# Up projections with both parts of x as one moving operand, and tiles placed at round addresses

## The chip, the cores and the metric

The kernel runs on one core of one Trainium2 chip. The metric is the device time of one execution in microseconds, the lower the better. A core has TensorE (PE in the profile; its weight loads are listed apart as PEld), VectorE (DVE), ScalarE (ACT), GpSimd (POOL) and SyncE (SP), which here only issues transfers. Each engine works through its own queue in order and waits on semaphores for the others.

## The reference: what is computed

Two layers of an encoder over 256 positions with 1024 channels, all in float32. Each layer has a token-mixing part (one input projection, a Hyena long convolution, a gated linear attention, a pooling mixer, three gated branch projections, one output projection, each with RMS norms around it) and a channel-mixing part. The change is in the channel-mixing part:

```python
h = _rms_norm(x, norm_ffn_pre[i])
a, b = _split(h @ ffn_w_up[i], (D_FF, D_FF))          # D_FF = 2816
a = _dwconv3_centred(a, ffn_conv_w[i], ffn_conv_b[i])  # three taps along the positions
y = (jax.nn.gelu(a, approximate=False) * b) @ ffn_w_down[i]
x = x + _rms_norm(y, norm_ffn_post[i])
```

## The kernel before

**Two parts of every number.** To keep float32 accuracy with TensorE's faster float32r format, each operand is cut into a high part (rounded to float32r) and a low part (what is left). A product then takes three matmuls: high by high, high by low, low by high (`mm3`, line 128).

**Weights.** All weight matrices are cut into 71 chunks a layer, each 128 partitions by 2048 numbers, 1 MB (line 31). SyncE loads them in the order of use into three raw buffers (`dma_next`, line 183). Each half of a chunk is split: ScalarE copies the high part into a slot (`split_upper`, line 205), VectorE subtracts it from the raw data to make the low part (`split_lower`, line 222); when both halves are done the raw buffer takes the next load. `filler` (line 246) splits ahead of use, as far as `ahead["chunks"]` and the free slots allow.

**Slots.** SBUF for passing data is a set of 37 big slots of 4096 bytes a partition (`b` in the profile) and 9 small ones of 2048 (`s`), PSUM is 8 banks (`p`); `Slots` (line 59) hands out the slot that has been free for the longest. The transposed and normalised activations, x, live in four big slots: two with the high and two with the low part, each for four blocks of 128 channels by 256 positions (`xt_alloc`, line 549). They are held while a layer's projections read them; `xt` is for token mixing, `xt2` for channel mixing, `xt3` for the next layer.

**The order of the work.** `unit` (line 320) emits the matmuls of one step, then the steps that empty the banks of the unit before it (`pending`), then lets the side work go on (`tick`) and splits weights ahead (`filler`). `cost` says how much side work a unit makes room for: 2.6 stands for one step. Side work beside the up projections of layer 0 is the Hyena filter of layer 1 (`filt`, line 467). A planner that simulates the engines puts the emitted instructions into each engine's order; in some windows the written order is kept (`open_window`, line 135).

**Up projections.** Line 1180 runs over 11 pairs in `UP_ORDER`; a pair is 256 channels of the gate path `a` and 256 of `b`. The `a` chunk goes through `two_ftiles` (line 576): two tiles of 128 output channels, one after the other in the two halves of one PSUM bank, each with 8 steps of the contraction and three matmuls in a step, weights stationary (128x128) and x moving (256 positions). Then `a_post` reads PSUM three times for each tile (`conv3`: one ScalarE step, two VectorE steps) and applies the GELU. For pairs 4 to 10 the `b` chunk goes the same way and `b_post` multiplies and splits. For pairs 0 to 3 the `b` channels come from four chunks computed just before the loop with x stationary, and are only transposed (line 1204). So each layer has 11 + 7 = 18 chunks through `two_ftiles` here; token mixing uses `two_ftiles` for other chunks, which the change leaves as they are. The down projection (line 1225) follows, with 512 moving columns of weights.

Of the kernel before, what the change touches and what calls it, by code (L numbers as in the profile page):

```python
# [12 lines left out]
F32 = mybir.dt.float32  # L13
# [70 lines left out]
@with_exitstack  # L84
def trunk(ctx: ExitStack, tc: tile.TileContext, a: dict, out: bass.AP):
    nc = tc.nc
    cpool = ctx.enter_context(tc.tile_pool(name="cst", bufs=1))
    wpool = ctx.enter_context(tc.tile_pool(name="wts", bufs=3))
    spool = ctx.enter_context(tc.tile_pool(name="slt", bufs=1))
    ppool = ctx.enter_context(tc.tile_pool(name="psm", bufs=1, space=bass.MemoryType.PSUM))  # L90
    big = Slots(spool, "b", 37, 4096)
    sml = Slots(spool, "s", 9, 2048)
    psm = Slots(ppool, "p", 8, 2048)

# [10 lines left out]
    def act(o, i, func=AF.Copy, **kw):  # L105
        ins = nc.scalar.activation(o, i, func, **kw)  # L106
        if func in TABLED:
            tc.stamp_issue_order_token(ins.ins, TOKEN)
# [10 lines left out]
    def mm(o, w, x, start, stop):  # L119
        ins = nc.tensor.matmul(o, w, x, start=start, stop=stop).ins  # L120
        if not isinstance(ins, tuple):
            newest["pe"] = ins
# [127 lines left out]
    def weights(n, at, width):  # L250

        half, at = divmod(at, 1024)
        return wh[n][half][:, at:at + width], wl[n][half][:, at:at + width]
# [39 lines left out]
    def start(gen, lift=0):  # L293
        s = Side(gen, lift)
        sides.append(s)
        return s

    def tick():
        for s in list(sides):
            s.step()  # L300
            if s.done:
                sides.remove(s)
# [244 lines left out]
    handles = {}  # L547

    def xt_alloc():
        return ([big.get([P, 4, L], F32R) for _ in range(2)], [big.get([P, 4, L], F32R) for _ in range(2)])  # L550

    def chunk_x_stationary(n, xt, t, o, half, first=None, lows_late=False):

# [14 lines left out]
            mm(o, x[:, k, s], l if m == 1 else h, half == 0 and (k, m) == todo[0], half == 1 and (k, m) == todo[-1])  # L568

    def ftile(n, xt, f, o, width=256, kn=8):  # L570
        xth, xtl = xt
        for k in range(kn):
            h, l = weights(n, k * width + f * P, P)
            mm3(o, h, l, xth[k // 4][:, k % 4, :], xtl[k // 4][:, k % 4, :], k == 0, k == kn - 1)

    def two_ftiles(n, xt, post):
        ps = psm.get([P, 2, L])
        unit([n], lambda: ftile(n, xt, 0, ps[:, 0, :]))

        def fin():  # L580
            post(ps)
            psm.put(ps)

        unit([n], lambda: ftile(n, xt, 1, ps[:, 1, :]), fin, free=n)
# [6 lines left out]
    def layer(i, xt, chains):  # L591
# [4 lines left out]
        def take():  # L596
            n = nxt()
            cur["c"] += 1
            return n
# [466 lines left out]
        def branch(b, ready):  # L1066
            for half in range(2):
                gate = room([P, 2, 512])
                if b == 0:
                    merged.append(gate)  # L1070
                n0, n1 = take(), take()
                for t in range(2):
                    ps = psm.get([P, 512])

                    def post(ps=ps, t=t, gate=gate):
                        act(gate[:, t, :], ps[:], AF.Sigmoid)
                        psm.put(ps)
                    for j, nj in enumerate((n0, n1)):
                        unit([nj, n1 if t else n0], lambda: chunk_x_stationary(nj, xt, t, ps[:], j),
                             post if j else None, free=nj if t else None)  # L1080
                ys = ready()
                n = take()
                if b == 2 and half == 1:
                    flush()
                    big.put(*xt[0], *xt[1])
                if b == 2:
                    mhl[half] = big.get([P, 4, L], F32R), big.get([P, 4, L], F32R)
                for t in range(2):
                    ps = psm.get([P, 512])

                    def post(ps=ps, gate=gate, half=half, t=t):
                        g, m = gate[:, t, :], merged[half][:, t, :]
                        tt(g, g, ps[:], ALU.mult)
                        psm.put(ps)
                        if b > 0:
                            tt(m, m, g, ALU.add)
                            if t == 1:
                                big.put(gate)
                        if b == 2:
                            later.append(lambda: merge_up(half, t))  # L1100

                    def pe(ps=ps, t=t):
                        s = slice(t * P, (t + 1) * P)
                        for k in range(4):
                            h, l = weights(n, k * 512, 512)
                            mm(ps[:], ys[0][:, k, s], h, k == 0, False)
                            mm(ps[:], ys[0][:, k, s], l, False, False)
                            mm(ps[:], ys[1][:, k, s], h, False, k == 3)
                    unit([n], pe, post, free=n if t else None)
# [29 lines left out]
        for t in range(2):  # L1139
            banks = [psm.get([P, 512]) for _ in range(2)]  # L1140
            ready = [False, False]
            ch2.append(start(post_norm(t, banks, g_post_t, g_pre2, *xt2, ready), LIFT))
            for c in range(4):
                def fin(ready=ready, c=c):
                    ready[c // 2] = True
                unit(ns[:c + 1] if t == 0 else ns[c:],
                     lambda: chunk_x_stationary(ns[c], mx, t, banks[c // 2][:], c % 2),
                     fin if c % 2 else None, free=ns[c] if t else None)
                if t == 0 and c == 2:
                    open_window()  # L1150
# [29 lines left out]
        for pair in UP_ORDER:  # L1180
            if pair // 2 not in ys_h:
                ys_h[pair // 2] = big.get([P, 4, L], F32R)
                ys_l[pair // 2] = big.get([P, 4, L], F32R)
            ga = sml.get([P, 2, L])

            def a_post(ps, pair=pair, ga=ga):
                for j in range(2):
                    conv3(ga[:, j, :], ps[:, j, :], i, V_FFC + 4 * (pair * 2 + j))
                act(ga[:], ga[:], AF.Gelu)

            def b_post(ps, pair=pair, ga=ga):
                tt(ga[:], ga[:], ps[:], ALU.mult)
                s = slice((pair % 2) * 2, (pair % 2) * 2 + 2)
                split(ys_h[pair // 2][:, s, :], ys_l[pair // 2][:, s, :], ga[:])
                sml.put(ga)
            two_ftiles(take(), xt2, a_post)
            if pair >= NB:
                two_ftiles(take(), xt2, b_post)
            else:
                ps = psm.get([P, 2, L])  # L1200
                for j in range(2):
                    f = (pair * 2 + j) * P
                    for t in range(2):
                        nc.tensor.transpose(ps[:, j, t * P:(t + 1) * P], bt[t][:, f:f + P], ident[:])  # L1204
                flush()

                def fin(ps=ps, b_post=b_post, pair=pair):
                    b_post(ps)
                    psm.put(ps)
                    if pair == NB - 1:  # L1210
                        big.put(*bt)
                pending.append(fin)
# [32 lines left out]
        for at, (t, c) in enumerate(seq):  # L1245
            if not done_first and c == 1:
                done_first = True
                flush()
                big.put(*xt2[0], *xt2[1])
                xt3 = xt_alloc() if not last else (None, None)  # L1250

            def fin(t=t):
                ch3.append(start(post_norm(t, banks[t], g_post2, None if last else g_cur["pre"], *xt3), LIFT))
            oldest = min(cc for _, cc in seq[at:])
            if t == 0 and c == 7 and not last:
                open_window()
            unit([ns[c], ns[oldest]], lambda: down(t, c), fin if c == 10 else None, free=ns[c] if t else None)
            if t == 1 and (c % 2 or c == 10):
                big.put(ys_h[c // 2], ys_l[c // 2])
        if last:  # L1260
            ready = [False, False]
            ch3.append(start(post_norm(1, banks[1], g_post2, None, *xt3, ready)))
            tail = [(half, c) for half in range(2) for c in range(11 - LEAD, 11)]
            for half, c in tail:
                def fin(half=half):
                    ready[half] = True
                unit([ns[c]], lambda: down(1, c, (half,)), fin if c == 10 else None, cost=1.3)
# [240 lines left out]
```

## Time and profile before

| | |
|---|---|
| time, median of 3 runs | 884.92 us (884.22 to 886.0) |
| the profiled execution | 884.6 us, its span 882.8 us |
| mean granted TensorE clock | 0.996 of full |
| matmuls, weight loads | 5381, 5381 |
| busy: TensorE, VectorE, ScalarE, GpSimd | 872.6, 636.0, 512.4, 37.4 us |
| read from HBM | 161.54 MB, 184 GB/s over the span |

A line of the profile names the engine, the line of the kernel (often that of a helper: L120 is every matmul, L106 every ScalarE step, L111 every VectorE step on two tensors, L114 every VectorE step with a scalar and two tensors, L374 and L1204 are transposes), the tiles written and read, the shapes, and how often it occurs. "Idle before" is the time in which the engine stood still ahead of these instructions, with what ended it. In tables by stretches each engine's busy time stands with the number of its instructions in brackets.

### The profile page before, as it was taken

How to read it: one execution, taken by the hardware profiler on the slowest of the kernel's cores; microseconds unless marked ns; L12 is line 12 of the kernel's file. 1: busy time of each engine (PE TensorE's matmuls, PEld its weight loads, DVE VectorE, ACT ScalarE, POOL GpSimd, SP SyncE). 2: the span in 40 equal slices, each digit the busy share in tenths (PEclk: the TensorE clock that was granted, in tenths of full speed). 3: DMA queues.
4: the chain of work that ended last, by engine and by line, in shares of the span. 5: the costliest groups of instructions: out<-in, count | busy, mean ns of one | idle time of the engine just before them, and what ended most of it. 6: DMA issues, size and time to landing. Idle time of an engine off the chain costs nothing.

```text
span 882.8 us, 13499 instructions
## 1 busy us (share of the span) xinstructions
PE 872.6 (99%) x5381; PEld 783.1 (89%) x5381; DVE 636.0 (72%) x925; ACT 512.4 (58%) x809; POOL 37.4 (4%) x86
## 2 busy tenths in 40 slices
PE   9999999999999999999999999999999999999997
PEld 7899987888888999998889999888888899999885
DVE  7899988766586798665288989876755967776612
ACT  7779666555365776554268865864543665555501
POOL 3000100000010000000010000000000000000000
PEclk9999999999999999999999999999999999999999
DMA  9854535746546446466349453465752674445501
GB/s 319 336 192 170 168 105 190 241 144 238 191 163 244 143 136 246 149 222 226 120 136 338 175 160 131 153 198 177 279 184 81 236 284 143 166 173 199 204 1 48
DMA packets 48431, 163.46 MB, mean 185 GB/s; under 512 B 3442, under 2 KB 29189, under 8 KB 33520
## 3 DMA queue, kind: packets, MB, share of 16 engines
q1 hardware_dynamic: 44352, 151.69, 49.2%
q0 software_dynamic: 4000, 10.90, 3.9%
q8 instruction: 42, 0.69, 0.3%
q14 instruction: 21, 0.17, 0.1%
q10 hardware_dynamic: 16, 0.00, 0.0%
HBM read 161.54 MB, written 1.05 MB: 184 GB/s over the span
## 4 chain that ended last, share of the span: by engine, by line
PE 96%; DVE 2%; DMA 1%; ACT 0%; issue 0%; SPq 0%; DVEq 0%; POOLq 0%; POOL 0%; ACTq 0%
PE p L120 94%; DVE b L111 1%; DMA raw<-in_wts 1%; PE p L374 1%; PE p L1059 0%; PE p L1204 0%; DMA x<-in_x 0%; ACT b L106 0%; PE p L775 0%; PE p L876 0%; PE p L1021 0%; DVE b L114 0%; DVE b L1281 0%; DVE s L111 0%; PE p L1294 0%
## 5 line engine op out<-in xcount | busy, mean ns | idle before, releaser
L120 PE MATMUL p<-b,b 128*128 128x256 f32 (+2 forms) x5022 | 842.1, 328 | 2.6 <-DVE b L111 1.9
L120 PEld LDWEIGHTS p<-b,b 128*128 128x128 f32 x5022 | 740.9, 190 | 85.6 <-DVE b L111 3.4
L111 DVE TENSOR_TENSOR b<-raw,b 128x1024 fp32r<-128x1024 f32 (+2 forms) x288 | 342.2, 1208 | 112.7 <-ACT b L106 55.2
L106 ACT ACTIVATE b<-raw 128x1024 fp32r<-128x1024 f32 (+2 forms) x290 | 292.0, 1041 | 159.3 <-PE p L120 128.3
L111 DVE TENSOR_TENSOR b<-p,b 128x512 f32<-128x512 f32 (+2 forms) x72 | 45.7, 654 | 66.5 <-ACT s L106 44.6
L106 ACT ACTIVATE b<-p 128x512 f32<-128x512 f32 (+3 forms) x90 | 50.1, 571 | 66.0 <-PE p L120 39.6
L106 ACT ACTIVATE s<-p 128x256 f32<-128x256 f32 (+3 forms) x50 | 20.3, 415 | 69.0 <-PE p L120 68.7
L114 DVE SCALAR_TENSOR_TENSOR s<-p,vec,s 128x255 f32<-128x255 f32 x104 | 49.3, 478 | 6.4 <-ACT s L106 5.5
L106 ACT ACTIVATE s<-p,vec 128x256 f32<-128x256 f32 x52 | 28.8, 558 | 19.0 <-DVE s L114 15.4
L106 ACT ACTIVATE s<-s 128x512 f32<-128x512 f32 (+6 forms) x54 | 29.0, 537 | 11.1 <-DVE s L111 5.6
L111 DVE TENSOR_TENSOR b<-s,b 128x512 fp32r<-128x512 f32 (+1 forms) x42 | 28.5, 685 | 6.0 <-ACT b L106 6.0
L106 ACT ACTIVATE b<-s 128x512 fp32r<-128x512 f32 x38 | 23.5, 625 | 9.6 <-DVE s L111 9.5
L111 DVE TENSOR_TENSOR b<-b,b 128x512 f32<-128x512 f32 (+4 forms) x28 | 22.4, 802 | 3.8 <-ACT b L106 3.3
L111 DVE TENSOR_TENSOR b<-b,p 128x512 f32<-128x512 f32 x24 | 16.2, 684 | 8.9 <-PE p L120 8.5
L111 DVE TENSOR_TENSOR s<-s,p 128x512 f32<-128x512 f32 x22 | 15.0, 683 | 8.1 <-ACT s L106 7.7
L106 ACT ACTIVATE b<-b,s 128x128 f32<-128x128 f32 x64 | 20.5, 395 | 0.0
L114 DVE SCALAR_TENSOR_TENSOR b<-p,vec,b 128x255 f32<-128x255 f32 (+1 forms) x40 | 19.1, 477 | 0.4 <-ACT b L106 0.3
L387 POOL TENSOR_TENSOR rstd<-mse,mhalf 128x1 f32<-128x1 f32 x16 | 8.9, 557 | 208.0 <-DVE mse L117 208.0
L106 ACT ACTIVATE b<-p,vec 128x256 f32<-128x256 f32 (+1 forms) x24 | 12.7, 530 | 8.1 <-PE p L120 5.8
L106 ACT ACTIVATE b<-b 1x512 f32<-1x512 f32 (+3 forms) x16 | 12.4, 780 | 4.1 <-DVE b L111 4.1
L106 ACT ACTIVATE s<-x 128x512 f32<-128x512 f32 x12 | 7.6, 633 | 11.6 <-DVE x L114 11.4
L164 POOL DMA_DIRECT2D b<-in_gains x7 | 3.9, 553 | 235.0 <-PE p L120 123.2
(108 smaller groups left out, 319.0 us busy)
## 6 DMA issues: line engine op xcount, KB each, us to landing
raw<-in_wts SPq DMA_DIRECT2D x116, 1024.0 KB, 4.9
raw<-in_wts SPq DMA_DIRECT2D x50, 512.0 KB, 4.7
b<-in_gains POOLq DMA_DIRECT2D x7, 512.0 KB, 4.9
b<-in_dft POOLq DMA_DIRECT2D x4, 512.0 KB, 5.4
raw<-in_wts SPq DMA_DIRECT2D x4, 256.0 KB, 5.4
b<-in_gw POOLq DMA_DIRECT2D x2, 512.0 KB, 6.1
b<-in_fw POOLq DMA_DIRECT2D x2, 512.0 KB, 7.3
b<-in_decay POOLq DMA_DIRECT2D x2, 512.0 KB, 7.6
```

The source lines that it names most:

```text
L106: ins = nc.scalar.activation(o, i, func, **kw)
L111: nc.vector.tensor_tensor(out=o, in0=x, in1=y, op=op)
L114: nc.vector.scalar_tensor_tensor(out=o, in0=x, scalar=s, in1=y, op0=op0, op1=op1)
L120: ins = nc.tensor.matmul(o, w, x, start=start, stop=stop).ins
L164: eng.dma_start(g[:], bass.AP(src.tensor, src.offset + (i * 4 + j) * DM, [[0, P], [1, DM]]))
L374: nc.tensor.transpose(ps[k // 4][:, k % 4, :], h[:, k * P:(k + 1) * P], ident[:])
L387: nc.gpsimd.tensor_tensor(out=r[:], in0=e[:], in1=mhalf[:, 0:1], op=ALU.pow)
```

## The change

The high and low part of x become one tile: for each block of 128 channels, 256 positions of the high part and then 256 of the low part lie side by side, 2 KB a partition. The two tiles that hold them come from a pool of their own and are no longer taken from the big slots, of which there are 33 instead of 37.

The 36 chunks of the up projections are computed by a wide form of `two_ftiles`. It takes two PSUM banks, one for each tile of output channels, and does the chunk in two units. The first has 16 matmuls of 512 moving columns: high weights by both parts of x, which land side by side in the bank. The second has 16 matmuls of 256 columns: low weights by the high part, added onto the first half of the bank. Then, for each tile, ScalarE copies the second half of the bank to a small slot and VectorE adds the first half to it; the convolution, GELU or product after it reads that slot and no longer PSUM.

Two unused tiles, of 384 and 256 bytes a partition, move the addresses: the tiles of x begin at multiples of 512 bytes and all slots at multiples of 2 KB.

```diff
@@ -84,11 +84,15 @@
+    xpool = ctx.enter_context(tc.tile_pool(name="xts", bufs=1))
+    xpool.tile([P, 96], F32, name="xpad")
     cpool = ctx.enter_context(tc.tile_pool(name="cst", bufs=1))
     wpool = ctx.enter_context(tc.tile_pool(name="wts", bufs=3))
+    apool = ctx.enter_context(tc.tile_pool(name="pad", bufs=1))
+    apool.tile([P, 64], F32, name="pad")
...
-    big = Slots(spool, "b", 37, 4096)
+    big = Slots(spool, "b", 33, 4096)
@@ -547,7 +551,10 @@
     def xt_alloc():
-        return ([big.get([P, 4, L], F32R) for _ in range(2)], [big.get([P, 4, L], F32R) for _ in range(2)])
+        ts = [xpool.tile([P, 4, 2, L], F32R, tag=f"xt{j}", name=f"xt{j}") for j in range(2)]
+        return ([t[:, :, 0, :] for t in ts], [t[:, :, 1, :] for t in ts], ts)
@@ -568,12 +575,44 @@
-    def two_ftiles(n, xt, post):
+    def ftiles_wide(n, xt, banks, lows):
+        for f, o in enumerate(banks):
+            for k in range(8):
+                h, l = weights(n, k * 256 + f * P, P)
+                x = xt[2][k // 4][:, k % 4]
+                if lows:
+                    mm(o[:, 0, :], l, x[:, 0, :], False, k == 7)
+                else:
+                    mm(o[:], h, x, k == 0, False)
+
+    def two_ftiles(n, xt, post, wide=False):
+        if wide:
+            c = 0
+            while not sml.free:
+                tick()
...
+            tmp = sml.get([P, 2, L])
+            banks = [psm.get([P, 2, L]) for _ in range(2)]
+
+            def out():
+                for f, ps in enumerate(banks):
+                    act(tmp[:, f, :], ps[:, 1, :])
+                    tt(tmp[:, f, :], tmp[:, f, :], ps[:, 0, :], ALU.add)
+                psm.put(*banks)
+                post(tmp)
+                sml.put(tmp)
+
+            unit([n], lambda: ftiles_wide(n, xt, banks, False), cost=3.6)
+            unit([n], lambda: ftiles_wide(n, xt, banks, True), out, cost=1.9, free=n)
+            return
@@ -1082,7 +1121,6 @@
-                    big.put(*xt[0], *xt[1])
@@ -1193,9 +1231,9 @@
-            two_ftiles(take(), xt2, a_post)
+            two_ftiles(take(), xt2, a_post, True)
             if pair >= NB:
-                two_ftiles(take(), xt2, b_post)
+                two_ftiles(take(), xt2, b_post, True)
@@ -1246,11 +1284,10 @@
-                big.put(*xt2[0], *xt2[1])
                 xt3 = xt_alloc() if not last else (None, None)
```

The rest of the diff passes only the first two members of `xt2` and `xt3` to the functions that write x.

More of the change, by code (lines that the diff above doesn't have):

```diff
@@ L570, in ftile @@
     def ftile(n, xt, f, o, width=256, kn=8):
-        xth, xtl = xt
+        xth, xtl = xt[:2]
         for k in range(kn):
@@ L574, in ftile @@
             mm3(o, h, l, xth[k // 4][:, k % 4, :], xtl[k // 4][:, k % 4, :], k == 0, k == kn - 1)
-    def two_ftiles(n, xt, post):
+    def ftiles_wide(n, xt, banks, lows):
[12 more added lines that the diff above has]
+                tick()
+                c += 1
+                assert c < 500, "no room"
+            tmp = sml.get([P, 2, L])
[10 more added lines that the diff above has]
+            return
         ps = psm.get([P, 2, L])
@@ L1141, in layer @@
             ready = [False, False]
-            ch2.append(start(post_norm(t, banks, g_post_t, g_pre2, *xt2, ready), LIFT))
+            ch2.append(start(post_norm(t, banks, g_post_t, g_pre2, *xt2[:2], ready), LIFT))
             for c in range(4):
@@ L1248, in layer @@
                 flush()
-                big.put(*xt2[0], *xt2[1])
                 xt3 = xt_alloc() if not last else (None, None)
             def fin(t=t):
-                ch3.append(start(post_norm(t, banks[t], g_post2, None if last else g_cur["pre"], *xt3), LIFT))
+                ch3.append(start(post_norm(t, banks[t], g_post2, None if last else g_cur["pre"], *xt3[:2]), LIFT))
             oldest = min(cc for _, cc in seq[at:])
@@ L1261, in layer @@
             ready = [False, False]
-            ch3.append(start(post_norm(1, banks[1], g_post2, None, *xt3, ready)))
+            ch3.append(start(post_norm(1, banks[1], g_post2, None, *xt3[:2], ready)))
             tail = [(half, c) for half in range(2) for c in range(11 - LEAD, 11)]
```

## The prediction

> **What bounds the kernel now.** I read the page first, then the chain of waits in order of time, then busy time by stretches, then the groups of instructions with their forms.
>
> ```profile
> PE 872.6 (99%) x5381; PEld 783.1 (89%) x5381; DVE 636.0 (72%) x925; ACT 512.4 (58%) x809; POOL 37.4 (4%) x86
> PEclk9999999999999999999999999999999999999999
> GB/s 319 336 192 170 168 105 190 241 144 238 191 163 244 143 136 246 149 222 226 120 136 338 175 160 131 153 198 177 279 184 81 236 284 143 166 173 199 204 1 48
> PE 96%; DVE 2%; DMA 1%; ACT 0%; issue 0%; SPq 0%; DVEq 0%; POOLq 0%; POOL 0%; ACTq 0%
> L120 PE MATMUL p<-b,b 128*128 128x256 f32 (+2 forms) x5022 | 842.1, 328 | 2.6 <-DVE b L111 1.9
> ```
>
> TensorE holds 96% of the chain, at 90% of full clock or more in every slice, and its main group waited for other engines for only 2.6 us in the whole span. So a microsecond taken out of TensorE's own stream is a microsecond of the kernel, as long as the other engines keep feeding it. A busy TensorE is not yet TensorE at its peak, so the pitch from one matmul to the next has to come from stretches that hold one form alone. The chain in order of time has such stretches in layer 1 (columns: start, length, engine and tile, count).
>
> ```profile
> 685.74 10.90 PE p L120 x48
> ...
> 734.70 0.44 PE p L1204 x4
> 735.13 17.28 PE p L120 x144
> 752.41 0.44 PE p L1204 x4
> 752.85 17.27 PE p L120 x144
> ```
>
> The first row is 48 matmuls with 512 moving columns: 10.90/48 = 227 ns each. The x144 rows are up projections, three chunks of 48 matmuls with 256 columns each, back to back between the transposes of L1204: 17.28/144 = 120 ns. From 256 to 512 columns the pitch grows by 107 ns, so 107 ns of each is columns, and both forms pay 13 ns beside them. That fixed part, once for each weight load with its matmul, is what the change can save.
>
> **TensorE's part of the change.** A chunk of up weights is two tiles of 128 output channels by 8 steps of the contraction. Now each step issues three pairs of 256 columns (high weights with the high part of x, high weights with the low part, low weights with the high part): 48 pairs, 48 x 120 = 5.76 us. Afterwards each step issues one pair of 512 columns (high weights, both parts) and one of 256 (low weights): 16 x 227 + 16 x 120 = 5.55 us. The columns streamed are the same; 16 weight loads with their fixed 13 ns are gone. That is 16 x 13 ns = 0.208 us a chunk. Each layer has 11 such chunks for the gate path and 7 for the other (pairs 4 to 10), 18 by 2 layers = 36, and 36 x 0.208 = **7.5 us** less. Bounds for the pitch of the wide pair, which reads x where today's 512-column pairs read weights: the lowest is its column part, the highest a slow stretch of 512-column pairs in the trace:
>
> ```profile
> 138.90 13.78 PE p L120 x60
> ```
>
> This is 229.7 ns, and at that pitch the gain falls by 576 x 2.7 ns = 1.6 us, to 5.9. I take 227, the row that holds in most stretches.
>
> The page "TensorE: Matmul & The Clock Gate" of the Trainium skill, section "Back-to-back issue gap", speaks against the change: warm, it gives N/2.4 + 2.5 ns, so a fixed part of 2.5 ns and not 13. By it a chunk would go from 5.24 to 5.20 us and the whole gain would be an estimated 1.5 us. The trace of this case disagrees by its 120 and 227 ns, and the sum goes by these.
>
> **What it adds on ScalarE and VectorE.** The two parts now stand side by side in a bank and have to be added: for each of the two tiles a ScalarE copy of 128x256 out of PSUM and a VectorE add of 128x256. The groups by form give the prices (busy us, mean ns):
>
> ```profile
> L106 ACT ACTIVATE s<-p 128x256 f32<-128x256 f32 x16 | 5.8, 384 | 3.8 <-PE p L120 3.6
> L111 DVE TENSOR_TENSOR b<-p,b 128x256 fp32r<-128x256 f32 x8 | 3.4, 420 | 5.4 <-ACT b L106 5.4
> L114 DVE SCALAR_TENSOR_TENSOR s<-p,vec,s 128x255 f32<-128x255 f32 x104 | 49.3, 478 | 6.4 <-ACT s L106 5.5
> L114 DVE SCALAR_TENSOR_TENSOR s<-b,b 128x256 f32<-128x256 f32 x8 | 3.1, 418 | 0.0
> L111 DVE TENSOR_TENSOR b<-raw,b 128x1024 fp32r<-128x1024 f32 x282 | 338.6, 1221 | 111.5 <-PE p L120 54.5 <-ACT b L106 54.0 <-issue 2.0
> ```
>
> So ScalarE gets 2 x 0.384 = 0.77 us a chunk and VectorE 2 x 0.420 = 0.84. A gate chunk gives back a little, since its four convolution steps read SBUF and no longer PSUM: 4 x (478 - 418) = 0.24 us. Both engines work behind TensorE here; the question is whether VectorE still splits the weights (2 x 1.22 us a chunk) in time. Busy time in the two halves of layer 0's up stage, and in two stretches of layer 1's:
>
> ```profile
> core 0: us, PE busy (x) PEld busy (x) DVE busy (x) ACT busy (x) POOL busy (x), PEclk, DMA share, GB/s
> 285.90:345.14 59.24, 59.24 (x473) 57.44 (x471) 52.51 (x80) 42.79 (x61) 0.52 (x1) 1.00 0.49 175
> 345.14:391.00 45.86, 45.86 (x385) 45.86 (x384) 30.02 (x41) 23.70 (x32) 1.06 (x2) 1.00 0.52 179
> 725.00:740.00 15.00, 15.00 (x127) 15.00 (x127) 11.30 (x18) 10.05 (x14) 0.00 (x0) 1.00 0.54 199
> 740.00:755.00 15.00, 15.00 (x128) 15.00 (x127) 9.76 (x13) 7.79 (x11) 0.00 (x0) 1.00 0.31 101
> ```
>
> Layer 1 and the second half of layer 0 have room: VectorE is at most 75% busy (11.30 of 15), and two to three chunks add at most 2.5 us to 15. The first half of layer 0's stage is tight, because the Hyena filter of layer 1 runs beside it: 52.51 of 59.24 us, 6.7 idle. Nine wide chunks end there, six of them gate chunks: + 9 x 0.84 - 6 x 0.24 = 6.1 us of VectorE, in a stretch that TensorE wants to leave 9 x 0.21 = 1.9 us earlier. If the 6.7 us of idle stay, VectorE comes out 6.1 + 1.9 = 8.0 us behind. **The cover** is the lead of the weight splits (instructions that touch the raw weights, from the start of the span):
>
> ```profile
> core 0: us, DVE busy (x) ACT busy (x), PEclk, DMA share, GB/s
> 0.00:326.30 326.30, 125.48 (x108) 109.10 (x110) 0.99 0.58 199
> ```
>
> and the chain where TensorE comes to these chunks:
>
> ```profile
> 329.35 15.60 PE p L120 x130
> ```
>
> The 108th VectorE split has just begun there. The 107 before it are 4 for the first chunk, 1 for the low-rank one and two for each of 51 more, so at 326.3 the tenth up chunk is ready (42 chunks stand before the up stage). TensorE begins the eighth at 329.35 and reaches the tenth two chunks later, at 329.35 + 2 x 5.76 = 340.9. This is the tightest place and the lead is 14.6 us. The 8.0 us fit in it, and the second half gives the lead back: 30.02 busy of 45.86, with 6 us added. The low weights, which VectorE makes last, are also needed later: all high pairs of a chunk come first now, 16 x 227 = 3.6 us of them. So I cost the additions at **nothing**; with the cover gone they cost the 8.0 us in full.
>
> Other edits with the answer nothing: a chunk holds two PSUM banks instead of one, of eight, and asks for the same pair again some four chunks (22 us) later, far behind a copy and add of 0.8 us a tile. The temporary takes one of nine small slots. Weights must come at 1 MB per 5.55 us, 189 GB/s, where the first slices moved 319 and 336; SyncE issues each transfer behind a split, so up to 8 us later in the tight half, and the same lead hides it. x leaves the big slots: 37 with 4 held become 33 with none held. For most of the program the free count is the same; between the last gate chunk and the output projection, and in the last down stage, it is four slots (one chunk) less. Layer 0's down stage already runs at the lower count, and its chain shows 256 matmuls of 512 columns without a wait:
>
> ```profile
> 390.98 57.63 PE p L120 x256
> ```
>
> 57.63/256 = 225 ns.
>
> **Alignment** (x at multiples of 512 bytes, slots at multiples of 2 KB) has no row: all slots stand at one remainder today, so no two stretches differ in it alone. Upper bound of a gain: the transposes of L1204 quoted above, from equally placed tiles, come at 0.44/4 = 110 ns, where 256-column pairs take 120. If each of the 5022 - 576 = 4446 remaining pairs shed 10 ns, that were 44 us. Lower bound: the 2.7 ns of the slow stretch on the 2616 wide pairs there will be, 7 us lost. I take zero: the 120 ns hold whichever tile feeds the pair, and the fixed part is the same for 1 KB and 2 KB of moving data, which boundaries crossed while streaming would not give.
>
> **The sum.** The profiled execution took 884.6 us (span 882.8 and 1.8 around it); the median shown is 884.92, 0.3 more, which the forecast leaves aside. 884.6 - 7.5 + 0 + 0 = **877.1 us**, 0.8% faster.
>
> **The rivals.**
>
> *The hand-overs starve the weights (slower).* Emptying a bank becomes two round trips between ScalarE and VectorE, each in order, with VectorE's weight splits queued behind an add that waits for a copy, and TensorE behind these splits. Such hand-overs cost about 1.0 us each today:
>
> ```profile
> ACT s L106 <- DVE s L114: 19.8, 20, 2.3
> ```
>
> Two for each of nine chunks add 18 us of idle VectorE in the tight half. With the 8.0 above it is 26 us behind, 11.4 more than the lead of 14.6; TensorE waits these and then runs at a reduced clock for a while, as after its one long wait today:
>
> ```profile
> 128.00:134.28 6.28, 4.52 (x21) 3.39 (x20) 6.28 (x10) 5.76 (x11) 0.00 (x0) 1.00 0.00 0
> 134.00:139.00 5.00, 4.72 (x14) 3.71 (x15) 4.99 (x10) 2.23 (x5) 0.00 (x0) 0.66 0.64 196
> ```
>
> The second row's clock of 0.66 loses 5 x 0.34 = 1.7 us. 877.1 + 11.4 + 1.7 = **890.2 us**. It decides from the point where VectorE falls more than 14.6 us behind. For it: VectorE is the fullest engine there. Against: the planner can put splits between the two halves.
>
> *A new wait somewhere.* The order of the work is planned anew; one wait like that at 128 us (6.28 - 4.52 = 1.76, and 1.7 of clock) costs 3.5: **880.6 us**. Against it: the emitted program is the same until the last branch of layer 0.
>
> *Packing saves nothing.* If the wide pair costs as much as two pairs, 240 ns, because the fixed part hangs on the operand and not on the pair, a chunk stays at 5.76 us: **884.6 us**. Against it: today's 512-column pairs take 227. The rule of the Trainium skill cited above ends near here, at 883.1.
>
> *Alignment shortens pairs.* A quarter of its bound, 11 us, gives **866 us**; the whole, 833. For it: the 13 ns have no explanation in the trace.
>
> **How the numbers follow.** Forecast 0.62; alignment 0.14; new wait 0.08; nothing saved 0.07; starved weights 0.09. A measurement of this kernel can tell about 0.2%, 1.8 us. Faster: 0.62 + 0.14 + 0.08 = 0.84; the same: 0.07; slower: 0.09. The range from 866 to 885 leaves out the starved case and some 0.1 of the alignment case. The forecast's own range is 875 to 879: the slow pitch of 229.7 on one side, some of the 13 ns saved with the other on the other.
>
> **What would show it.** Right: up chunks of 32 matmuls in 5.55 us, the main TensorE group with 576 fewer at no more than 3 us idle, down stage and token mixing at 227 and 120 ns as before, VectorE near 95% between 286 and 345 us with splits still ahead. Wrong: gaps before the up matmuls released by VectorE, a clock below 1.00 there, or a pitch other than 227 and 120 in stages that the change does not touch, which would be the alignment.

## The result, and the profile after

The changed kernel takes 878.15 us (median of 4 runs, 876.59 to 879.6); the kernel before, run beside it, 884.86 us (884.22 to 886.0). The ratio is 0.9927, with a 95% interval from 0.9912 to 0.9942: 0.7% faster, 6.7 us by the medians. The forecast was 877.1 us. The profiled execution took 877.21 us, its span is 874.5 us.

The first part of the page of the changed kernel, and the shares of its chain:

```profile
PE 863.9 (99%) x4805; PEld 751.5 (86%) x4805; DVE 657.5 (75%) x997; ACT 534.0 (61%) x881; POOL 37.4 (4%) x86
...
PE 96%; DVE 2%; DMA 1%; ACT 0%; issue 0%; SPq 0%; DVEq 0%; POOLq 0%; POOL 0%; ACTq 0%
```

TensorE still holds 96% of the chain. It has 576 matmuls fewer, and its busy time fell by 8.7 us, about as much as the span. VectorE and ScalarE each have 72 instructions and some 21.5 us more; none of that lengthened the span.

Where the time went is read from the chain of waits in order of time (start, length, engine and line, count). After:

```profile
134.45 16.77 PE p L124 x72
...
264.05 20.00 PE p L124 x94
...
342.07 101.72 PE p L124 x508
...
680.93 10.90 PE p L124 x48
...
712.39 16.71 PE p L124 x96
```

and three rows of before that the prediction does not show:

```profile
134.28 18.40 PE p L120 x72
...
265.48 20.23 PE p L120 x110
...
345.38 103.23 PE p L120 x636
```

Going down the two lists side by side:

- At 264.05 and 265.48 us both kernels begin the last stretch ahead of layer 0's up stage; its end already holds the first wide chunk (94 pairs for 110, 0.23 us less). The changed kernel is 1.43 us ahead here, before a single wide pair has run. The reason is the row that starts at 134 us: the same 72 matmuls took 16.77 us after and 18.40 before. This is no work of the change; the last section comes back to it.
- When ten of layer 0's up chunks are done (342.07 against 345.38), it is 3.31 us ahead. At 680.93 against 685.74, with all of layer 0's up stage passed, it is 4.81.
- At the end of the span it is 874.5 against 882.8, 8.3 us ahead. Of these 1.43 came before the up stage; 8.3 - 1.43 = 6.9 us came from the 36 chunks.

A chunk's price is read where nothing else runs on TensorE: three chunks up to a row of transposes took 17.28 us before (144 pairs) and take 16.71 now (96 pairs), so 5.76 and 5.57 us. 36 x 0.19 = 6.8 us, which is what the list gives.

The groups by form show the pairs in their new shapes, and the steps added on the other engines (busy us, mean ns | idle before):

```profile
L124 PE MATMUL p<-b,xt 128*128 128x512 f32 x960 | 230.6, 393 | 2.6 <-DVE b L115 2.2 <-ACT b L110 0.4
...
L124 PE MATMUL p<-xt,b 128*128 128x512 f32 x576 | 139.4, 392 | 0.0
L118 DVE SCALAR_TENSOR_TENSOR s<-s,vec,s 128x255 f32<-128x255 f32 x88 | 39.8, 478 | 5.2 <-ACT s L110 5.0
L110 ACT ACTIVATE s<-p 128x256 f32<-128x256 f32 x88 | 32.1, 376 | 23.6 <-PE p L124 23.1
L115 DVE TENSOR_TENSOR s<-s,p 128x256 f32<-128x256 f32 x72 | 28.5, 414 | 3.3 <-ACT s L110 3.2
```

The 576 wide pairs waited for nothing (0.0). TensorE's 2.6 us of idle time stand before the same kind of matmul as ahead of the change, outside the up stages. The adds cost 414 ns and the copies 376. The convolution steps now read SBUF and still take 478 ns from start to end; since one may start while the last one ends, 88 of them make VectorE busy for 39.8 us, 452 ns each.

Busy time in the two halves of layer 0's up stage (columns as in the prediction):

```profile
284.26:342.07 57.81, 57.81 (x328) 50.02 (x327) 51.92 (x89) 44.79 (x73) 0.52 (x1) 1.00 0.47 164
342.07:387.00 44.93, 44.93 (x260) 39.62 (x259) 40.80 (x68) 32.88 (x57) 1.06 (x2) 1.00 0.60 211
```

The first half is as full as before: 5.9 us of VectorE idle, where there were 6.7. What did not fit went to the second half, 40.80 busy of 44.93 where it was 30.02 of 45.86. The weight splits alone, from the start of the span (VectorE's busy time and their number, then clock, DMA share, GB/s):

```profile
0.00:323.60 323.60, 125.55 (x107) 1.00 0.58 200
```

At 323.60 us 107 splits are done, so the tenth chunk is ready. TensorE begins the ninth at 330.26, where the chain has its next long piece:

```profile
330.26 11.37 PE p L124 x66
```

It reaches the tenth at 330.26 + 5.57 = 335.8. The lead in the tightest place is now about 12 us.

The 14.6 us of the prediction for the kernel before came of a misreading: TensorE doesn't begin the eighth chunk at 329.35, it is in the middle of it. The row there has 130 matmuls and ends with the tenth chunk, so 96 of them are the ninth and the tenth, and 34 are the rest of the eighth. The tenth is reached after 34 + 48 = 82 matmuls, at 329.35 + 82 x 0.120 = 339.2, and the lead before was 339.2 - 326.3 = 12.9 us. So the additions took less than 1 us from it.

### The profile page after: what moved, and what is told of

Its sections match the earlier page's. It is cut to its first block, busy times and chain, and to the rows that moved or that the text cites. A ratio compares the mean times of both kernels' runs of the same rounds, so it can differ in the third digit from the quotient of the medians.

```text
span 874.5 us, 12489 instructions
## 1 busy us (share of the span) xinstructions
PE 863.9 (99%) x4805; PEld 751.5 (86%) x4805; DVE 657.5 (75%) x997; ACT 534.0 (61%) x881; POOL 37.4 (4%) x86
## 4 chain that ended last, share of the span: by engine, by line
PE 96%; DVE 2%; DMA 1%; ACT 0%; issue 0%; SPq 0%; DVEq 0%; POOLq 0%; POOL 0%; ACTq 0%
PE p L124 94%; DVE b L115 1%; DMA raw<-in_wts 1%; PE p L378 1%; PE p L1098 0%; PE p L1242 0%; DMA x<-in_x 0%; ACT b L110 0%; PE p L814 0%; PE p L1060 0%; PE p L915 0%; DVE b L1318 0%; DVE s L115 0%; DVE xt L118 0%; PE p L1331 0%
## 5 line engine op out<-in xcount | busy, mean ns | idle before, releaser
L124 PE MATMUL p<-xt,b 128*128 128x256 f32 (+1 forms) x2336 | 352.5, 310 | 0.0
L124 PEld LDWEIGHTS p<-xt,b 128*128 128x128 f32 x2336 | 324.2, 191 | 26.3 <-issue 1.0
L124 PE MATMUL p<-b,b 128*128 128x512 f32 (+1 forms) x1150 | 267.8, 385 | 0.0
L124 PEld LDWEIGHTS p<-b,b 128*128 128x128 f32 x1150 | 209.4, 188 | 40.9 <-issue 0.3
L124 PE MATMUL p<-b,xt 128*128 128x512 f32 x960 | 230.6, 393 | 2.6 <-DVE b L115 2.2
L124 PEld LDWEIGHTS p<-b,xt 128*128 128x128 f32 x960 | 178.0, 188 | 41.2 <-DVE b L115 3.5
L110 ACT ACTIVATE s<-p 128x256 f32<-128x256 f32 (+3 forms) x122 | 46.6, 391 | 83.4 <-PE p L124 82.8
L118 DVE SCALAR_TENSOR_TENSOR s<-s,vec,s 128x255 f32<-128x255 f32 x88 | 39.8, 478 | 5.2 <-ACT s L110 5.0
L115 DVE TENSOR_TENSOR s<-s,p 128x256 f32<-128x256 f32 (+1 forms) x80 | 33.6, 440 | 4.5 <-ACT s L110 4.3
L110 ACT ACTIVATE s<-s,vec 128x256 f32<-128x256 f32 x44 | 24.6, 592 | 3.3 <-DVE s L115 3.3
```

Of the source, the lines that this page charges most:

```text
L115: nc.vector.tensor_tensor(out=o, in0=x, in1=y, op=op)
L118: nc.vector.scalar_tensor_tensor(out=o, in0=x, scalar=s, in1=y, op0=op0, op1=op1)
```

## The experiments

Two theories stood against each other at first. **Fewer pairs**: the gain is the fixed 13 ns of each weight load with its matmul, 576 times, and the additions are hidden. **Alignment**: the round addresses make pairs shorter, and the wide form does little or is paid for by its additions. After that the question was how much cover the additions really have, and whether the same form pays elsewhere. The runs were made in three groups, each beside the kernel before, which took 883.73, 884.54 and 885.34 us: the first four rows, the next four, the last three. The ratio is taken from all executions of a group, so it can differ a little from that of the medians.

| run | median, us | ratio to before, 95% |
|---|---|---|
| the changed kernel again | 878.74 | 0.9938 (0.9923 to 0.9953) |
| without the two unused tiles | 877.72 | 0.9931 (0.9914 to 0.9947) |
| before, with the slots moved | 885.1 | 1.0008 (0.9997 to 1.0019) |
| wide pairs cut into pairs of 256 | 885.08 | 1.0008 (0.9998 to 1.0018) |
| two more VectorE steps per tile | 879.59 | 0.9951 (0.9936 to 0.9966) |
| four more VectorE steps per tile | 899.56 | 1.0174 (1.0157 to 1.0191) |
| wide form in token mixing too | 889.5 | 1.0059 (1.0039 to 1.008) |
| the same, layer 1 alone | 883.46 | 0.9995 (0.9985 to 1.0006) |
| the same, GpSimd adds | 883.55 | 0.9982 (0.9969 to 0.9994) |
| GpSimd adds, both layers | 892.46 | 1.009 (1.0072 to 1.0109) |
| wide pairs of 384 columns | 853.73 (one run) | leaves work out |

### Is it the pairs or the addresses?

Four kernels on one chip, where the kernel before took 883.73 us. The first is the changed kernel once more.

> The changed kernel once more, beside the runs below. All theories: about 878 us, 6 to 8 us below the kernel before.

It gave 0.9938, and its interval overlaps that of the first measurement. By the medians it is 5.0 us below the kernel before, a little less than the 6 to 8 expected; its profile lost some clock near the start, which the last section shows.

The second takes the two unused tiles out of the changed kernel, so that x and the slots stand at other remainders again:

```diff
-    xpool.tile([P, 96], F32, name="xpad")
...
-    apool = ctx.enter_context(tc.tile_pool(name="pad", bufs=1))
-    apool.tile([P, 64], F32, name="pad")
```

> The changed kernel without the two unused tiles: x begins at 128 past a multiple of 512 bytes, the slots at 1408 past a multiple of 2 KB, as before the change. Packing alone (my theory): the gain stays, 877 to 879 us, pitches 120 and 227 ns. Alignment (rival): a visible part of the gain goes, 880 us or more, and the pitch of wide pairs is over 227 ns.

The third moves the slots of the kernel before to multiples of 2 KB and does nothing else:

```diff
+    apool = ctx.enter_context(tc.tile_pool(name="pad", bufs=1))
+    apool.tile([P, 160], F32, name="pad")
```

> The kernel before with one unused tile of 640 bytes ahead of the slots, so that all slots, x among them, begin at multiples of 2 KB; nothing is packed. Packing alone (my theory): no change, 884 to 886 us. Alignment (rival): faster by 2 us or more, with pairs shorter than 120 and 227 ns.

The chain of the second has the same three chunks at the price of the changed kernel:

```profile
712.42 16.71 PE p L121 x96
```

and the chain of the third has them at the price of the kernel before:

```profile
735.72 17.27 PE p L122 x144
```

With the pads gone nothing is lost (0.9931), and alone they bring nothing (1.0008). The alignment theory falls.

The fourth keeps everything of the changed kernel, the two banks, the copies and the adds, and cuts each wide pair into two of 256 columns with a weight load each:

```diff
-                    mm(o[:], h, x, k == 0, False)
+                    mm(o[:, 0, :], h, x[:, 0, :], k == 0, False)
+                    mm(o[:, 1, :], h, x[:, 1, :], False, False)
```

> The changed kernel with each wide pair of 512 columns issued as two pairs of 256 with the same weights into the same halves of the bank: 48 pairs a chunk again, the copies and additions stay. My theory (13 ns for each pair, additions hidden by the lead of the weight splits): all of the gain goes and no more, 884 to 886 us, 120 ns a pair in the up stages. Rival (the additions cost time that the packing covers): slower than the kernel before, 887 us or more, with TensorE waiting for VectorE between 285 and 345 us.

Its chain has the three chunks so:

```profile
716.32 17.28 PE p L124 x144
```

and its busy time in the first half of layer 0's up stage is this:

```profile
285.90:345.14 59.24, 59.24 (x470) 57.46 (x469) 55.27 (x95) 47.70 (x76) 0.52 (x1) 1.00 0.48 175
```

The three chunks are back at 17.28 us and the ratio at 1.0008, from 0.9998 to 1.0018. The whole gain hangs on the number of pairs. The same run prices the additions: VectorE has all of them (55.27 us busy here, 52.51 before), and the time is that of the kernel before. They cost nothing that can be measured.

### What the fixed part follows

Two widths cannot tell a fixed cost for each pair from one that grows with the width in another way. A third can. This kernel cuts the wide pairs to 384 columns; its expectation says what that leaves out.

```diff
-                    mm(o[:], h, x, k == 0, False)
+                    flat = lambda ap: ap.rearrange("p a b -> p (a b)")[:, 0:384]
+                    mm(flat(o[:]), h, x.rearrange("p a b -> p (a b)")[:, 0:384], k == 0, False)
...
-                    act(tmp[:, f, :], ps[:, 1, :])
+                    act(tmp[:, f, 0:128], ps[:, 1, 0:128])
+                    act(tmp[:, f, 128:256], ps[:, 1, 0:128])
```

> The changed kernel with the wide pairs cut to 384 columns: the product of the high weights with the low part of x is left out for the last 128 positions (the copy takes columns 0 to 127 twice). Theory (a fixed 13 ns beside 107 ns for 256 columns): 160 + 13 = 173 ns a wide pair, 16 x 173 + 16 x 120 = 4.69 us a chunk, so 36 x 0.86 = 31 us less, about 847 us. Rival (a pair below 512 columns costs more than its columns): over 180 ns.

In its chain, three chunks of 16 wide and 16 narrow pairs:

```profile
719.22 14.09 PE p L124 x96
```

48 narrow pairs take 48 x 0.120 = 5.76 us, so a pair of 384 columns takes (14.09 - 5.76)/48 = 173.5 ns. The three widths lie on one line: 120, 173.5 and 227 ns, 53.5 ns for each 128 columns and 13 ns beside them. The fixed part belongs to the pair.

The whole run came to 853.73 us, some 7 above what was expected. Part of it went ahead of the up stage: the 72 matmuls that begin at 134.45 us in the profile of the changed kernel begin at 136.98 here. The rest goes with a wait. The waits between 284 and 330 us (waited for: us in total, times, longest):

```profile
PE p L124 <- DVE s L115: 3.5, 1, 3.5
```

Busy time around it, and the instructions in order of time (start, length, engine, and the idle time before it with what ended it):

```profile
303.00:307.00 4.00, 0.54 (x6) 0.34 (x4) 1.44 (x4) 3.16 (x5) 0.00 (x0) 0.86 0.93 348
307.00:312.00 5.00, 5.00 (x13) 4.23 (x14) 4.82 (x10) 3.36 (x11) 0.00 (x0) 0.50 0.02 8
```

```profile
303.79 1.28 ACT L110 ACT_TABLE_LOAD   x1
...
305.75 1.15 DVE L115 TENSOR_TENSOR s<-s,s 128x512 f32<-128x512 f32 x2 [2.42 <-ACT s L110]
...
306.95 1.65 PE L124 MATMUL p<-b,s 128*128 128x512 f32 x3 [3.46 <-DVE s L115]
```

TensorE waited 3.5 us for a small slot that VectorE writes, and then ran 5 us at half clock. VectorE itself was mostly idle (1.44 of 4.00): it waited 2.42 us for ScalarE, which had just loaded a table. The matmul that waited (p<-b,s, no tile of x) is one of the Hyena filter of layer 1: what came late was a step of the side work, not a weight. Whether the shorter stream outran its cover, or the 72 additional ScalarE copies of this kernel (953 steps for 881) held the side work up, this one run doesn't tell.

### How much cover do the additions have?

The prediction took the lead of the weight splits as the whole cover and put 8.0 us of delay under it. To find where the cover ends, two or four VectorE steps that change nothing (the maximum of a number with itself) go behind each add:

```diff
                     tt(tmp[:, f, :], tmp[:, f, :], ps[:, 0, :], ALU.add)
+                    for _ in range(2):
+                        tt(tmp[:, f, :], tmp[:, f, :], tmp[:, f, :], ALU.max)
```

> The changed kernel with two more VectorE steps of 128x256 (a maximum of a value with itself) behind each addition: 4 x 0.42 = 1.7 us more VectorE work in each wide chunk, the numbers computed stay the same. In the changed kernel VectorE is busy for 92.7 of the 102.7 us of layer 0's up stage and for 79.8 of 95.7 us of layer 1's. My theory (the lead of the weight splits, 13 us at its tightest, hides additions until it is used up): layer 0 gets 17 x 1.7 = 29 us more, 19 beyond its stage, so TensorE waits for some 6 us there, with 1 to 2 us of reduced clock; layer 1 gets 30 us more, 14 beyond its stage, within its lead of 22. 882 to 888 us. Rival (no lead that counts, each added microsecond that doesn't fit is waited for): 19 + 14 us, 910 us or more. Rival (VectorE is no bound at all): 878 us.

> As e4_two_more with four more VectorE steps behind each addition: 3.4 us more in each wide chunk. My theory: beyond the lead every microsecond counts, layer 0 is 47 us over and waits for about 34, layer 1 is 44 over and waits for about 22: 930 us, within 15. Rival (VectorE is no bound): 878 us.

A maximum takes 416 ns, and by that two for each of two tiles were to be 1.7 us a chunk. But steps on SBUF overlap at their ends: over the whole run VectorE is busy for 700.4 us where the changed kernel has 657.5, so the 36 chunks got 42.9 us, 1.2 us each, and nine chunks 11 us. If each of them came out of the lead of about 12 us, next to nothing would be left of it. The time was 879.59 us against 878 to 879, below the 882 to 888 that I expected. TensorE has one wait from 200 us on:

```profile
PE p L124 <- ACT b L110: 0.8, 1, 0.8
```

Busy time in the two halves of the up stage and in the 23 us behind them:

```profile
284.00:342.00 58.00, 57.16 (x319) 48.77 (x318) 55.48 (x109) 41.23 (x68) 0.52 (x1) 1.00 0.41 146
342.00:387.00 45.00, 45.00 (x263) 39.75 (x262) 43.63 (x85) 29.24 (x52) 1.06 (x2) 1.00 0.51 187
387.00:410.00 23.00, 23.00 (x107) 19.20 (x106) 23.00 (x42) 14.17 (x19) 0.00 (x0) 1.00 0.64 229
```

The last of these stretches in the changed kernel:

```profile
387.00:410.00 23.00, 23.00 (x103) 19.05 (x102) 13.01 (x14) 11.64 (x13) 0.00 (x0) 1.00 0.52 183
```

VectorE took less idle time in the up stage (2.5 and 1.4 us in place of 6.2 and 4.1), and the rest ran on into the down stage, where it is busy 23.00 of 23.00 us instead of 13.01. The groups of these 23 us say with what: with weight splits as before, and with steps on chunks whose matmuls were already done, eight convolution steps among them, where the changed kernel has none.

```profile
L118 DVE SCALAR_TENSOR_TENSOR s<-s,vec,s 128x255 f32<-128x255 f32 x8 | 3.7, 478 | 0.0
```

The lead of the splits fell by far less than 11 us: the 107th split ends at 327.7 and the tenth chunk begins at 337.3, 9.6 us later. So the cover is wider than I took it: it also holds the steps on finished banks, which may lag behind TensorE, and the down stage is there to catch up.

Four maxima add 747.8 - 657.5 = 90.3 us of VectorE in all, 2.5 us a chunk, and are over the edge: 899.56 us. The waits from 200 us on:

```profile
PE p L124 <- DVE s L115: 12.1, 7, 5.6
...
PE p L124 <- DVE b L115: 0.6, 1, 0.6
```

and the busy time in two stretches of layer 0:

```profile
355.00:368.00 13.00, 6.86 (x37) 5.69 (x36) 13.00 (x32) 6.53 (x12) 0.00 (x0) 0.91 0.38 148
367.00:371.00 4.00, 3.71 (x9) 2.97 (x10) 4.00 (x12) 1.36 (x4) 0.00 (x0) 0.50 0.01 4
```

VectorE is full (13.00 of 13.00) and TensorE stands still, 12.1 us in seven waits over both layers, and in between half the clock is gone for a while (0.50): the same 4805 matmuls keep TensorE busy for 872.7 us instead of 863.9. I expected some 930 us, and the loss is 21 us over the changed kernel, so most of the 90.3 us is still hidden. Of note is what is waited for: VectorE steps on the small slot, the ones that read the banks and so empty them. Waits for the low weights (the row with b) come to 0.6 us, and the splits keep their lead: the 107th ends at 332.0 and the tenth chunk begins at 344.0. So here, with VectorE too full, it was the emptying of the banks that stopped TensorE, not the weight splits. Where the added work stands has a part in that: the maxima come between the adds that empty the two banks of a chunk.

### Does the form pay in token mixing?

The same form, used for the 24 `two_ftiles` chunks of token mixing too, would save 24 x 0.19 = 4.6 us more. The temporary is taken from the big slots there.

```diff
+            slots = big if wide == "b" else sml
...
-        two_ftiles(take(), xt, hy_post("x1", 0))
+        two_ftiles(take(), xt, hy_post("x1", 0), "b")
...
-        two_ftiles(take(), xt, qk_post(eb, 0, float(P ** -0.5)))
+        two_ftiles(take(), xt, qk_post(eb, 0, float(P ** -0.5)), "b")
```

> The changed kernel with the wide form also for the 24 chunks of token mixing that go through the two-tile function (Hyena, queries, keys, pooling), with the temporary in a big slot. TensorE's stream gets 24 x 0.2 = 4.8 us shorter. My theory: in layer 1 this shows, in layer 0 VectorE is full between 50 and 135 us (48.5 of 50 us in one stretch) and TensorE already waits for it once, so 12 x 0.84 = 10 us more VectorE work costs up to 10 us there: 874 to 886 us, with a longer wait near 130 us. Rival (only the number of pairs counts): 873 us.

It is slower than before, 889.5 us and 1.0059, and above the 874 to 886 that I expected. Its waits from 20 us on:

```profile
PE p L124 <- ACT b L110: 5.5, 5, 1.9
PE p L124 <- DVE b L115: 2.5, 3, 1.7
PE p L124 <- DVE s L115: 1.8, 1, 1.8
```

Of the changed kernel the same view has one row:

```profile
PE p L124 <- DVE b L115: 1.8, 1, 1.8
```

These three rows, the largest, make 9.8 us of waits against 1.8: the 8.0 us that are new outweigh the 4.6 saved. The net of 3.4 us is not the whole loss against the changed kernel, 10.8 us. The rest shows as TensorE's busy time, which rose from 863.9 to 866.4 us with 384 matmuls fewer; the clock has a part in it (0.995 in the mean for 0.998), and how large a part was not worked out. Since the first waits come early in layer 0, the next kernel does it in layer 1 only (12 chunks, 2.3 us to save):

```diff
-        two_ftiles(take(), xt, hy_post("x1", 0))
+        two_ftiles(take(), xt, hy_post("x1", 0), i == 1 and "b")
...
```

> As e6_all_wide, with the wide form of token mixing in layer 1 alone, where VectorE is busy for about 44 of 50 us and TensorE doesn't wait: 12 x 0.2 = 2.4 us off, 875.5 us. Rival (VectorE's additions delay the chain of the mixers): 878 us or more.

Also wrong: I expected 875.5, and it took 883.46 us, some 5 us more than the changed kernel and no less than the kernel before (0.9995). Busy time of this kernel in layer 1's token mixing:

```profile
500.00:525.00 25.00, 25.00 (x145) 22.09 (x144) 24.44 (x47) 20.50 (x49) 1.42 (x2) 1.00 0.51 165
525.00:550.00 25.00, 23.99 (x137) 20.70 (x135) 23.83 (x46) 13.83 (x23) 1.34 (x9) 1.00 0.27 86
550.00:575.00 25.00, 22.35 (x108) 17.98 (x106) 20.95 (x34) 18.31 (x31) 0.00 (x0) 0.93 0.59 189
```

and of the changed kernel:

```profile
500.00:525.00 25.00, 25.00 (x201) 24.57 (x200) 20.41 (x37) 15.30 (x35) 1.60 (x3) 1.00 0.49 147
525.00:550.00 25.00, 25.00 (x194) 24.26 (x193) 23.86 (x41) 14.20 (x24) 1.09 (x9) 1.00 0.40 129
550.00:575.00 25.00, 25.00 (x129) 21.23 (x128) 22.04 (x34) 20.51 (x30) 0.00 (x0) 1.00 0.47 158
```

In the changed kernel VectorE has 4.6 us to spare in the first of these stretches and 1.1 in the second. The additions use up what is left, TensorE loses 1.0 and then 2.65 us of busy time, and after the waits some clock (0.93). The chain of this kernel ahead of the longest wait also holds a weight transfer of 5.40 us, from 550.73, that SyncE issued behind a VectorE step that ended at 550.29.

If VectorE is the limit, another engine could do the adds. In the next two kernels ScalarE copies the whole bank to a big slot and GpSimd adds the halves, in layer 1 and in both layers:

```diff
...
+                    if slots is big:
+                        act(both[:, f], ps[:])
+                        nc.gpsimd.tensor_tensor(out=both[:, f, 0, :], in0=both[:, f, 0, :], in1=both[:, f, 1, :], op=ALU.add)
+                        continue
...
```

> As e7_layer1_wide, but in the 12 wide chunks of token mixing ScalarE copies a whole bank (128x512) and GpSimd, which is 4% busy, adds the two halves in SBUF, so VectorE gets no additions. Theory (e7 lost because VectorE was full): the waits between 545 and 580 us go and the shorter stream shows, 875 to 877 us. Rival (the longer way out of the bank delays the mixers' chains, whichever engine adds): 880 us or more, with TensorE waiting for ScalarE or GpSimd.

> The same in both layers: 24 chunks of token mixing wide, with the additions on GpSimd. Theory (VectorE alone was the trouble): 872 to 875 us. Rival (layer 0's chain near 130 us is bound by ScalarE and the order of the chain as well): 880 us or more, as e6_all_wide or worse, since ScalarE copies 128x512 and no longer 128x256.

883.55 and 892.46 us: not clearly better than with VectorE in layer 1 alone (0.9982 for 0.9995, and the intervals overlap), and no better in both layers. Both theories fell, and both times are those of the rivals, 880 us or more. In layer 1 TensorE's one wait in token mixing is for ScalarE, 3.1 us at 551.95, and the chain ahead of it is mostly VectorE's. The groups by form there show what became of VectorE's room. With VectorE adding, a step with two inputs in SBUF:

```profile
L118 DVE SCALAR_TENSOR_TENSOR b<-b,vec,b 128x255 f32<-128x255 f32 x16 | 7.0, 476 | 0.0
```

With GpSimd adding, the same step and the adds:

```profile
L118 DVE SCALAR_TENSOR_TENSOR b<-b,vec,b 128x255 f32<-128x255 f32 x16 | 9.5, 618 | 0.1
...
L611 POOL TENSOR_TENSOR b<-b 128x256 f32<-128x256 f32 x24 | 25.7, 1078 | 60.7 <-ACT b L110 60.7
```

A GpSimd add takes 1078 ns for VectorE's 411 to 414. And VectorE's own steps get longer, here from 476 to 618 ns in the mean. That it goes with the adds can be seen inside this run, in the order of time: the same step (L121, one tensor with scalars) once with no add beside it, once beside one.

```profile
485.42 0.42 DVE L121 TENSOR_SCALAR s<-s 128x512 f32<-128x512 f32 x1
...
489.95 1.50 POOL L611 TENSOR_TENSOR b<-b 128x256 f32<-128x256 f32 x1 [0.17 <-ACT b L110]
490.78 0.96 DVE L121 TENSOR_SCALAR s<-s 128x512 f32<-128x512 f32 x1
```

VectorE was to lose 0.8 us a chunk, and stays just as full:

```profile
525.00:550.00 25.00, 23.84 (x135) 20.62 (x133) 24.40 (x35) 12.08 (x20) 10.98 (x18) 1.00 0.35 106
```

"SBUF — State Buffer" of the Trainium skill, section "Who interferes with whom", says that VectorE and GpSimd share one pair of ports into SBUF, and that a VectorE step with two inputs in SBUF contends with a GpSimd step that reads there. The longer steps with two inputs in SBUF agree with it; the step of L121 has one input, and this rule doesn't speak of it. No run here takes the contention alone away, so how much of the loss it makes, how much the slower add and how much ScalarE's longer copies stays open.

No version in these runs beats the changed kernel. The one without the two unused tiles equals it and is simpler.

## Why the prediction was right, and where not

**What bounds the kernel, and the pitch: right.** TensorE's stream set the time, and the gain is the number of pairs times their fixed part. Predicted were 0.208 us a chunk and 7.5 us; it was 0.19 a chunk, and 6.9 us by the chain. The size is off by 8%: with 48 narrow pairs at 120 ns as before, the wide pair comes to (16.71 - 5.76)/48 = 228 ns, 1 ns above the 227 taken from 512-column pairs with x stationary and inside the bound of 229.7. Cutting the pairs again gave back the whole gain.

**The 2.5 ns a pair of the Trainium skill: disagreed with.** "TensorE: Matmul & The Clock Gate" of the Trainium skill, section "Back-to-back issue gap", left some 1.5 us of gain as an estimate. The section gives the 2.5 ns for the gap of an isolated matmul, and the prediction took it for a stream of weight loads with their matmuls; for such a stream the section has 131 ns at 512 columns. Neither agrees with the trace, where such pairs take 227 ns. Three widths now give 13 ns beside 53.5 ns for each 128 columns. What the 13 ns are, the runs do not say, nor whether the load or the matmul has them: every matmul here comes with its own load.

**The additions at nothing: right in the result, the cover named too narrowly.** The run with 256-column pairs shows that they cost nothing. I named the lead of the splits, read it as 14.6 us where it was 12.9, and put 8.0 us of it to use; it shrank by less than 1, and 11 us more of VectorE work cost about 1 us. So the 8.0 us did not come out of that lead. What I left out is the second store: steps on finished banks can lag, into the down stage, where VectorE is only 13.01 of 23.00 us busy. For the same reason "VectorE near 95%" in the first half did not come true: 51.92 of 57.81 is 90%, and the second half took the rest.

**Convolution steps that read SBUF: wrong row.** The term "4 x (478 - 418) = 0.24 us" of a gate chunk took the price of a step without a tensor of scalars (`vec`); with one, the step takes 478 ns from SBUF as from PSUM. What VectorE really got is less than the whole term made it all the same: its busy time rose by 657.5 - 636.0 = 21.5 us, where 36 x 0.84 - 22 x 0.24 = 25.0 us were predicted. Steps that overlap at their ends (452 ns of busy time for 478) go some way to explain it. This size lies under the cover and did not reach the time.

**Alignment at zero: right**, and better than it was argued: with and without it, two kernels each agree within 0.1% by their ratios. The 14% given to it as a rival, and the range down to 866 with it, were paid for by an unexplained 13 ns; a run that moves the addresses alone settled it. The bound of 10 ns a pair was taken from transposes, which move 128 columns, against pairs of 256, so it compared two forms and not two places.

**Starved weights: right to be unlikely, wrong in its mechanism.** It was to decide when VectorE falls more than 14.6 us behind, with two hand-overs of about 1.0 us in each chunk. The hand-overs cost next to nothing: VectorE stood idle for 3.3 us in all ahead of the 72 adds. With 11 us added to nine chunks starvation did not appear. With 2.5 us a chunk, 23 us in nine, TensorE did wait, but for banks to be emptied (12.1 us), hardly for weights (0.6).

**A new wait somewhere: did not come**; the wait near 130 us is the same 1.8 us in both kernels, and the idle time of the main group is 2.6 us still. **Packing saves nothing**: refuted by 5.57 us a chunk.

The forecast for the profiled execution, 877.1 us, hit 877.21 partly by luck: 6.9 us came from the chunks and 1.43 from a clock that was not lost this time, and the time around the span was 877.21 - 874.5 = 2.7 us where the forecast kept 1.8. By the medians the gain is 6.7 us.

## What to carry to other kernels

Where TensorE sets the time and each matmul comes with its own weight load, price the pitch at two widths from rows that hold one form alone; what doesn't grow with the width is what merging two matmuls under one weight load saves. The merged form moves the adding to VectorE, so it pays only in stages where VectorE has spare time now or can catch up soon after: the same edit gained 0.7% beside the up projections and lost more than that in the token mixing of both layers. Where cover is the question, load it on purpose until it breaks, and look at what is waited for then.

## What the runs showed of the hardware

**A wait of 2 us costs clock in some executions and not in others.** Both kernels have the same wait near 132 us, 1.8 us long. Before, the clock in the 5 us after it was 0.66 (in the prediction). After:

```profile
134.45:139.50 5.05, 5.05 (x22) 4.19 (x23) 5.04 (x10) 2.55 (x5) 0.00 (x0) 1.00 0.70 213
```

It stays at 1.00, though the wait is the same, and this makes the difference of 1.6 us in the row at 134 us. In the second profile of the changed kernel the clock fell elsewhere, near the start:

```profile
12.00:20.00 8.00, 8.00 (x32) 6.86 (x33) 6.96 (x19) 7.33 (x17) 4.79 (x9) 0.79 0.91 309
```

Its span is 876.9 us, 2.4 above the first, and 8 x 0.21 = 1.7 us of that is the clock of this row; the first profile has 1.00 there. So two profiles of one kernel differ by a quarter of this change's gain from the clock alone, and the profile of before that I started from had such a loss in it. Compare spans stage by stage, by chain rows at the same place, before a difference of 1 to 2 us is given to an edit. What decides whether the clock falls is open.

**Addresses did not matter** to TensorE's pitch here: with the slots at multiples of 2 KB and away from them, 256-column pairs come at 120 ns and chunks of wide pairs at 5.57 us.

**A VectorE step with a tensor of scalars took 478 ns** whether it read PSUM or SBUF; 128x256 without one took 418 (rows in the prediction). That the scalars are the reason is only read from these rows; no run changed that alone.
